# Accumulator sums by ScalarE copies and accumulating DMAs, and more seven-product places, in a hybrid encoder layer's feed-forward part

## The chip, the cores and the metric

One core of a Trainium2 chip runs the whole layer as one program. The metric is the device time of one execution in microseconds. Engines: TensorE (PE) multiplies, VectorE (DVE) and ScalarE (ACT) do elementwise work, GpSimd (POOL) and SyncE (SP) here mostly issue DMAs or do little.

## The reference

One layer on 256 tokens of width 2048 in float32. An RMSNorm and an input projection feed a gated linear recurrence and a differential attention, whose outputs go through W_out to the residual. The part that the change touches is what follows:

```python
h = rmsnorm(x, norm_ffn_w[l])
u = jax.nn.silu(jnp.einsum('bsd,df->bsf', h, w_gate[l])) * jnp.einsum('bsd,df->bsf', h, w_up[l])
x = x + jnp.einsum('bsf,fd->bsd', u, w_down[l])
```

The inner width D_FF is 5632, that is 11 chunks of 512 columns.

## The kernel before

**Products in split precision.** Every weight tile of 128x1024 float32 (two slices of 128 rows by 512 columns, a "unit") is split into a high part `whi`, a rounded copy by ACT (L134), and a rest `wlo` by a DVE subtraction (L135). Activations are split likewise, and each product is three matmuls of 128x128 by 128x512: hi by hi, hi by lo, lo by hi (L772 to L774). The class `Stream` loads units with DMAs on SP's queue into `raw` (5 buffers), and splits them in a fixed order of `items`, up to three items ahead of use, five in the feed-forward part (`HL_BUFS` and `HL_MORE` buffers). Splits have high priority in the planner, which simulates the program to fix the order on each engine.

**Seven products in place of eight.** In the feed-forward part two chunks of columns (gate and up of a chunk f; two neighbouring chunks of down) are multiplied together by `pair_product`. The contraction is done in places i of two 128-row slices. A plain place has 2 chunks x 2 halves of tokens x 2 slices = 8 products, 24 matmuls. A place named in `S_UP` or `S_DOWN` uses seven products (21 matmuls), from sums of the activations, made once, and sums of the weights: four DVE operations of 128x512 (L127, L128, L131, L132) and, besides the first unit, one half unit and two units more to split, all made in place in `raw`. Some products go to accumulators x (one per chunk and half of tokens), others to the four accumulators m, which are added to several x results at the end. Places up to the last seven come in order of i for both chunks; the remaining plain places come for chunk 0 and then for chunk 1.

**Accumulators.** The four x and four m fill all eight PSUM banks. `new_pair_accs` swaps roles from one pair to the next, so that the next pair starts in banks that m held, while x is taken out of the others.

**fold** runs after the last seven of a pair. For gate and up it forms the four sums of m into the SBUF tiles u and v: an ACT copy of m[0] (L862) and four DVE additions (L863 to L866). At the chunk's end DVE adds x[0] into u (L870), ACT takes Silu (L871), DVE adds x[1] into v (L873) and multiplies (L874). For down, fold adds the sums to the residual `xsb` with an ACT copy and eight DVE additions (L888, L890), and four more add x at the end (L903); in the second phase the result is stored from there.

**put_u** is a generator in a queue `side`, which `pump` moves on by one step after every second product. It regroups u: two DVE transposes (L405), four stores to a DRAM tile `via`, `settle(2)` (it yields until two more items are taken), one load to `ut`, a longer settle, then the split into u_hi (ACT, L836) and u_lo (DVE, L838) and the activation sums for the places in `S_DOWN` (L719 to L728). `put_sums` does the latter for the places in `S_UP` at the start of the feed-forward part. `acts.wait(i)` pumps until place i is ready.

**Phases.** Chunks 0 to 5 of gate and up, then down over their 12 places, for two pairs of column chunks; then chunks 6 to 10 and down over their 10 places.

Of the kernel before, what the change touches and what calls it, by code (L numbers as in the profile page):

```python
# [11 lines left out]
F32 = mybir.dt.float32  # L12
F32R = mybir.dt.float32r
BF16 = mybir.dt.bfloat16
U8 = mybir.dt.uint8
AF = mybir.ActivationFunctionType
ALU = mybir.AluOpType
# [3 lines left out]
P = 128  # L21
SEQ = 256
TT = SEQ // P
NC = 512
# [10 lines left out]
RAW_BUFS, HL_BUFS, HAT_BUFS = 5, 3, 5  # L35
HL_MORE = 2
PHASES = 2
S_UP = (2, 4)
S_DOWN = ((1, 3, 5, 7), (1, 3, 5))
EVERY_IN, EVERY_OUT, EVERY_FFN, WIDTH = 1, 1, 2, 2  # L40
LB_FLOOR = 1e-30
LB_CEIL = 1.0 - 1e-6
LEVELS = [1, 2, 4, 8, 16, 32, 64]
# [8 lines left out]
def encoder_layer(ctx: ExitStack, tc: tile.TileContext, xT, xr, w_in, w_out, w_gate, w_up, w_down,  # L52
# [188 lines left out]
            stream.split(upto)  # L241


    ident = const.tile([P, P], F32, name="ident")
    make_identity(nc, ident)
    nhalf = const.tile([P, 8], F32, name="nhalf")
    nc.gpsimd.memset(nhalf, -0.5)
    dist_sb = const.tile([P, TT, SEQ], F32, name="dist_sb")
    masks_sb = const.tile([P, len(LEVELS), P], U8, name="masks_sb")
    vec = const.tile([P, params.shape[1]], F32, name="vec")  # L250
    nfw = vec[:, 0:NK]
    onw, qnw, kn1, slw = (vec[:, NK + i:NK + i + 1] for i in range(4))
# [137 lines left out]
    def settle(n):  # L390

        u = stream.at
        for _ in range(2 * HPC * n):
            yield
            if stream.at >= u + n:
                break
# [428 lines left out]
    nkp = max(len(p) for p in phases) * HPC  # L825
    n_down = max(len(s) for s in S_DOWN)

    def put_u(f, u, ph, u_hi, u_lo, us_hi, us_lo, ready):

        tmp, ut = (ffn.tile([P, NQ, HPC, TT, Q], F32, tag="ut", name=n) for n in ("uq", "ut"))  # L830
        yield from regroup(ut, u, tmp)
        k0 = (f - phases[ph][0]) * HPC
# [18 lines left out]
    for ph, fs in enumerate(phases):  # L851
# [3 lines left out]
        for f in fs:  # L855
            x, m = new_pair_accs()
            u = ffn.tile([P, TT, NC], F32, tag="u", name="u")
            v = ffn.tile([P, TT, NC], F32, tag="v2", name="v", bufs=1)

            def fold():  # L860
                tt = nc.vector.tensor_tensor
                nc.scalar.copy(out=u[:, 0, :], in_=m[0])  # L862
                tt(out=u[:, 1, :], in0=u[:, 0, :], in1=m[2], op=ALU.add)  # L863
                tt(out=v[:, 0, :], in0=u[:, 1, :], in1=m[1], op=ALU.add)
                tt(out=u[:, 1, :], in0=u[:, 1, :], in1=m[3], op=ALU.add)
                tt(out=v[:, 1, :], in0=u[:, 1, :], in1=m[1], op=ALU.add)  # L866

            pair_product(up_plan[f], h_acts, x, m, EVERY_FFN, fold)
            for tt in range(TT):
                nc.vector.tensor_tensor(out=u[:, tt, :], in0=u[:, tt, :], in1=x[0][tt], op=ALU.add)  # L870
                nc.scalar.activation(out=u[:, tt, :], in_=u[:, tt, :], func=AF.Silu, scale=rstd2[:, tt:tt + 1])  # L871
            for tt in range(TT):
                nc.vector.tensor_tensor(out=v[:, tt, :], in0=v[:, tt, :], in1=x[1][tt], op=ALU.add)  # L873
                nc.vector.scalar_tensor_tensor(out=u[:, tt, :], in0=v[:, tt, :], scalar=rstd2[:, tt:tt + 1],  # L874
                                               in1=u[:, tt, :], op0=ALU.mult, op1=ALU.mult)
            side.append(put_u(f, u, ph, u_hi, u_lo, us_hi, us_lo, ready))

        u_acts = Acts(u_hi, u_lo, us_hi, us_lo, S_DOWN[ph])
        u_acts.ready = ready
        for cp in range(NCH_D // 2):  # L880
# [1 line left out]
            xs = [[xsb[:, tt, (2 * cp + c) * NC:(2 * cp + c + 1) * NC] for tt in range(TT)] for c in range(2)]  # L882

            def fold():
                t = ffn.tile([P, NC], F32, tag="v2", name="t", bufs=1)

                def add(to, what):
                    nc.vector.tensor_tensor(out=to, in0=to, in1=what, op=ALU.add)  # L888

                nc.scalar.copy(out=t, in_=m[0])  # L890
                add(xs[0][0], t)
                add(t, m[2])
                add(xs[1][0], t)
                add(xs[1][0], m[1])
                add(t, m[3])
                add(xs[0][1], t)
                add(xs[1][1], t)
                add(xs[1][1], m[1])

            pair_product(down_plan[ph, cp], u_acts, x, m, EVERY_FFN, fold)  # L900
            for c in range(2):
# [58 lines left out]
```

## Time and profile before

| | |
|---|---|
| median of 3 runs | 1227.65 us (1225.65 to 1227.96) |
| the profiled execution | 1226.58 us, its span 1224.5 us |
| PE busy | 1211.1 us (99%), 5553 matmuls |
| DVE busy | 985.9 us (81%) |
| ACT busy | 707.9 us (58%) |
| POOL busy | 38.0 us (3%) |
| DMA | 252.51 MB, mean 206 GB/s |

The span is cut into stretches to read it: the mixing part runs until about 520 us, chunks of gate and up until 778, down until 902, chunks again until 1119, and down until the end. A group's mean time is one instruction's own duration; DVE starts the next before the last has drained, so the distance between two starts is shorter.

### The profile page before, as it was taken

The numbers are of one execution on the slowest core, as the hardware profiler recorded it, in microseconds if no ns is written. First come the engines' busy times: TensorE is split into PE (matmuls) and PEld (weight loads), VectorE is DVE, ScalarE is ACT, GpSimd is POOL, SyncE is SP. The second block draws the span as 40 slices with busy tenths as digits, with TensorE's granted clock in tenths as the row PEclk, the third lists the DMA queues.
The fourth block names the chain that finished last, engine by engine and source line by source line (L and its number), as shares of the span: only waits on it lengthen the run. The fifth ranks groups of instructions, "written<-read, shape, count | busy, mean of one in ns | idle before, by whom it ended". The sixth has DMA issues, their size and how long they took to land.

```text
span 1224.5 us, 15730 instructions
## 1 busy us (share of the span) xinstructions
PE 1211.1 (99%) x5553; PEld 1000.5 (82%) x5553; DVE 985.9 (81%) x1413; ACT 707.9 (58%) x1029; POOL 38.0 (3%) x42
## 2 busy tenths in 40 slices
PE   9999999999999999999999999999999999999998
PEld 6878888887888788878888888888888888888887
DVE  6558977756987776698998988898978989888885
ACT  6657756776775665565554565464545545654542
POOL 0000111000001100000000000000000000000000
PEclk9999999999999999999999999999999999999999
DMA  8965456566445554547666675665657666766763
GB/s 308 314 229 179 150 174 205 189 211 202 149 147 186 190 184 161 188 139 255 240 201 216 227 253 196 222 223 185 216 196 239 203 212 229 253 197 222 232 208 120
DMA packets 79934, 252.51 MB, mean 206 GB/s; under 512 B 8944, under 2 KB 19824, under 8 KB 79856
## 3 DMA queue, kind: packets, MB, share of 16 engines
q1 hardware_dynamic: 79712, 251.52, 61.4%
q8 instruction: 43, 0.70, 0.2%
q14 instruction: 35, 0.29, 0.1%
q10 hardware_dynamic: 144, 0.01, 0.0%
HBM read 238.38 MB, written 13.11 MB: 205 GB/s over the span
## 4 chain that ended last, share of the span: by engine, by line
PE 85%; DMA 6%; DVE 4%; ACT 2%; issue 1%; SPq 1%; POOL 0%; ACTq 0%; DVEq 0%
PE x L773 15%; PE x L774 15%; PE x L772 15%; PE acc L377 9%; PE acc L378 9%; PE acc L376 9%; PE sc L493 2%; PE m L773 2%; PE m L774 2%; PE m L772 2%; DVE wlo L135 2%; DMA zt<-via 2%; DMA raw<-in_w_in 2%; ACT whi L134 1%; DMA ut<-via 1%
## 5 line engine op out<-in xcount | busy, mean ns | idle before, releaser
L134 ACT CAST whi<-raw 128x1024 fp32r<-128x1024 f32 (+1 forms) x497 | 498.2, 1018 | 392.0 <-PE x L774 123.2
L135 DVE TENSOR_TENSOR wlo<-raw,whi 128x1024 fp32r<-128x1024 f32 (+1 forms) x497 | 578.9, 1180 | 156.0 <-ACT whi L134 152.6
L774 PE MATMUL x<-whi,h_lo 128*128 128x512 f32 x594 | 231.2, 389 | 0.0
L773 PE MATMUL x<-wlo,h_hi 128*128 128x512 f32 x594 | 231.1, 389 | 0.0
L772 PE MATMUL x<-whi,h_hi 128*128 128x512 f32 x594 | 220.4, 389 | 0.0
L377 PE MATMUL acc<-wlo,h_hi 128*128 128x512 f32 x512 | 203.2, 397 | 2.9 <-DVE wlo L135 2.9
L378 PE MATMUL acc<-whi,h_lo 128*128 128x512 f32 x512 | 200.4, 393 | 0.0
L376 PE MATMUL acc<-whi,h_hi 128*128 128x512 f32 x512 | 193.5, 399 | 2.6 <-ACT whi L134 2.5
L772 PEld LDWEIGHTS x<-whi,h_hi 128*128 128x128 f32 x594 | 111.5, 188 | 23.3 <-ACT whi L134 0.2
L773 PEld LDWEIGHTS x<-wlo,h_hi 128*128 128x128 f32 x594 | 111.5, 188 | 23.3
L774 PEld LDWEIGHTS x<-whi,h_lo 128*128 128x128 f32 x594 | 111.5, 188 | 23.1
L377 PEld LDWEIGHTS acc<-wlo,h_hi 128*128 128x128 f32 x512 | 96.8, 189 | 24.3 <-DVE wlo L135 6.1
L376 PEld LDWEIGHTS acc<-whi,h_hi 128*128 128x128 f32 x512 | 96.1, 189 | 22.6 <-ACT whi L134 4.2
L378 PEld LDWEIGHTS acc<-whi,h_lo 128*128 128x128 f32 x512 | 96.7, 189 | 19.3
L773 PE MATMUL x<-wlo,u_hi 128*128 128x512 f32 x282 | 109.8, 389 | 0.0
L774 PE MATMUL x<-whi,u_lo 128*128 128x512 f32 x282 | 109.7, 389 | 0.0
L772 PE MATMUL x<-whi,u_hi 128*128 128x512 f32 x282 | 105.1, 390 | 0.4 <-ACT whi L134 0.4
L772 PEld LDWEIGHTS x<-whi,u_hi 128*128 128x128 f32 x282 | 52.6, 188 | 12.4 <-ACT whi L134 1.6
L773 PEld LDWEIGHTS x<-wlo,u_hi 128*128 128x128 f32 x282 | 52.9, 188 | 11.3 <-DVE wlo L135 0.4
L774 PEld LDWEIGHTS x<-whi,u_lo 128*128 128x128 f32 x282 | 52.9, 188 | 10.9
L377 PE MATMUL acc<-wlo,m_hi 128*128 128x512 f32 x128 | 50.2, 393 | 0.5 <-DVE wlo L135 0.5
L378 PE MATMUL acc<-whi,m_lo 128*128 128x512 f32 x128 | 49.9, 390 | 0.0
(192 smaller groups left out, 1289.9 us busy)
## 6 DMA issues: line engine op xcount, KB each, us to landing
raw<-in_w_in SPq DMA_DIRECT2D x127, 512.0 KB, 4.2
raw<-in_w_gate SPq DMA_DIRECT2D x88, 512.0 KB, 4.7
raw<-in_w_up SPq DMA_DIRECT2D x88, 512.0 KB, 4.7
raw<-in_w_down SPq DMA_DIRECT2D x88, 512.0 KB, 4.7
raw<-in_w_out SPq DMA_DIRECT2D x32, 512.0 KB, 4.0
via<-uq SPq DMA_DIRECT2D x44, 128.0 KB, 2.4
ut<-via SPq DMA_DIRECT2D x11, 512.0 KB, 3.3
via<-zq SPq DMA_DIRECT2D x40, 128.0 KB, 3.7
```

What stands on the lines that cost most here:

```text
L134: nc.scalar.copy(out=hi[:, k, :], in_=raw[:, k, :])
L135: self.last_split = tt(out=lo[:, k, :], in0=raw[:, k, :], in1=hi[:, k, :].bitcast(F32), op=ALU.subtract)
L376: nc.tensor.matmul(out=acc, lhsT=hi, rhs=whi[:, k, :], start=first, stop=False)
L377: nc.tensor.matmul(out=acc, lhsT=hi, rhs=wlo[:, k, :], start=False, stop=False)
L378: nc.tensor.matmul(out=acc, lhsT=lo, rhs=whi[:, k, :], start=False, stop=last)
L493: nc.tensor.matmul(out=sc[:, j, :], lhsT=kk[:, j * P:(j + 1) * P], rhs=qq(j), start=True, stop=True)
L772: nc.tensor.matmul(out=acc, lhsT=hi, rhs=whi[:, k, :], start=first, stop=False)
L773: nc.tensor.matmul(out=acc, lhsT=hi, rhs=wlo[:, k, :], start=False, stop=False)
L774: nc.tensor.matmul(out=acc, lhsT=lo, rhs=whi[:, k, :], start=False, stop=left[id(acc)] == 0)
```

## The change

More places use seven products: `S_UP` goes from (2, 4) to (1, 3, 5), `S_DOWN` from (1, 3, 5, 7) and (1, 3, 5) to (1, 3, 5, 7, 9) and (1, 3, 5, 7). In fold of gate and up, ACT copies m[1] into both halves of v; DVE makes two sums; two accumulating DMAs on POOL's queue add them into v. At the chunk's end ACT copies x[0] to a new tile xg and one accumulating DMA adds it into u. Silu and the multiplication move into put_u, behind a new settle(2). In down's fold four DVE additions remain and four accumulating DMAs add the sums to `xsb`. Three constant tiles move to the pool `mixp`, whose memory the feed-forward pool takes over.

```diff
-S_UP = (2, 4)
-S_DOWN = ((1, 3, 5, 7), (1, 3, 5))
+S_UP = (1, 3, 5)
+S_DOWN = ((1, 3, 5, 7, 9), (1, 3, 5, 7))
...
-    ident = const.tile([P, P], F32, name="ident")
+    ident = mixp.tile([P, P], F32, name="ident")
...
-    dist_sb = const.tile([P, TT, SEQ], F32, name="dist_sb")
-    masks_sb = const.tile([P, len(LEVELS), P], U8, name="masks_sb")
+    dist_sb = mixp.tile([P, TT, SEQ], F32, name="dist_sb")
+    masks_sb = mixp.tile([P, len(LEVELS), P], U8, name="masks_sb")
...
-    def put_u(f, u, ph, u_hi, u_lo, us_hi, us_lo, ready):
+    def put_u(f, u, v, ph, u_hi, u_lo, us_hi, us_lo, ready):
+        yield from settle(2)
+        for tt in range(TT):
+            rs = rstd2[:, tt:tt + 1]
+            with tc.issue_after(stream.last_split.ins):
+                nc.scalar.activation(out=u[:, tt, :], in_=u[:, tt, :], func=AF.Silu, scale=rs)
+            nc.vector.scalar_tensor_tensor(out=u[:, tt, :], in0=v[:, tt, :], scalar=rs, in1=u[:, tt, :],
+                                           op0=ALU.mult, op1=ALU.mult)
+            yield
...
             def fold():
                 tt = nc.vector.tensor_tensor
+                t = ffn.tile([P, NC], F32, tag="sm", name="t")
                 nc.scalar.copy(out=u[:, 0, :], in_=m[0])
-                tt(out=u[:, 1, :], in0=u[:, 0, :], in1=m[2], op=ALU.add)
-                tt(out=v[:, 0, :], in0=u[:, 1, :], in1=m[1], op=ALU.add)
-                tt(out=u[:, 1, :], in0=u[:, 1, :], in1=m[3], op=ALU.add)
-                tt(out=v[:, 1, :], in0=u[:, 1, :], in1=m[1], op=ALU.add)
+                for c in range(2):
+                    nc.scalar.copy(out=v[:, c, :], in_=m[1])
+                tt(out=t, in0=u[:, 0, :], in1=m[2], op=ALU.add)
+                tt(out=u[:, 1, :], in0=t, in1=m[3], op=ALU.add)
+                nc.gpsimd.dma_start(out=v[:, 0, :], in_=t, accum_op=ALU.add)
+                nc.gpsimd.dma_start(out=v[:, 1, :], in_=u[:, 1, :], accum_op=ALU.add)
             pair_product(up_plan[f], h_acts, x, m, EVERY_FFN, fold)
+            xg = ffn.tile([P, TT, NC], F32, tag="ut", name="xg")
             for tt in range(TT):
-                nc.vector.tensor_tensor(out=u[:, tt, :], in0=u[:, tt, :], in1=x[0][tt], op=ALU.add)
-                nc.scalar.activation(out=u[:, tt, :], in_=u[:, tt, :], func=AF.Silu, scale=rstd2[:, tt:tt + 1])
+                nc.scalar.copy(out=xg[:, tt, :], in_=x[0][tt])
+            nc.gpsimd.dma_start(out=u, in_=xg, accum_op=ALU.add)
             for tt in range(TT):
                 nc.vector.tensor_tensor(out=v[:, tt, :], in0=v[:, tt, :], in1=x[1][tt], op=ALU.add)
-                nc.vector.scalar_tensor_tensor(out=u[:, tt, :], in0=v[:, tt, :], scalar=rstd2[:, tt:tt + 1],
-                                               in1=u[:, tt, :], op0=ALU.mult, op1=ALU.mult)
...
             def fold():
-                t = ffn.tile([P, NC], F32, tag="v2", name="t", bufs=1)
...
-                nc.scalar.copy(out=t, in_=m[0])
-                add(xs[0][0], t)
-                add(t, m[2])
-                add(xs[1][0], t)
-                add(xs[1][0], m[1])
-                add(t, m[3])
-                add(xs[0][1], t)
-                add(xs[1][1], t)
-                add(xs[1][1], m[1])
+                t = ffn.tile([P, 2, NC], F32, tag="v2", name="t12", bufs=1)
+                t3 = ffn.tile([P, NC], F32, tag="sm", name="t3")
+                tt = nc.vector.tensor_tensor
+                nc.scalar.copy(out=t[:, 0, :], in_=m[0])
+                tt(out=t[:, 1, :], in0=t[:, 0, :], in1=m[2], op=ALU.add)
+                tt(out=t3, in0=t[:, 1, :], in1=m[3], op=ALU.add)
+                for c in range(2):
+                    tt(out=xs[1][c], in0=xs[1][c], in1=m[1], op=ALU.add)
+                for to, what in ((xs[0][0], t[:, 0, :]), (xs[1][0], t[:, 1, :]), (xs[0][1], t3), (xs[1][1], t3)):
+                    nc.gpsimd.dma_start(out=to, in_=what, accum_op=ALU.add)
```

## Rows read from the trace of the kernel before

**Rows 1.** The page: its head and the busy time of each engine.

```profile
span 1224.5 us, 15730 instructions
PE 1211.1 (99%) x5553; PEld 1000.5 (82%) x5553; DVE 985.9 (81%) x1413; ACT 707.9 (58%) x1029; POOL 38.0 (3%) x42
```

**Rows 2.** Busy time by stretch (columns in the first line): gate/up chunk, down pattern, down product.

```profile
core 0: us, PE busy (x) PEld busy (x) DVE busy (x) ACT busy (x) POOL busy (x), PEclk, DMA share, GB/s
567.19:609.35 42.16, 42.16 (x187) 34.91 (x186) 37.90 (x48) 22.87 (x26) 0.00 (x0) 1.00 0.67 227
...
778.00:818.80 40.80, 40.59 (x179) 33.05 (x178) 37.45 (x44) 22.04 (x25) 0.00 (x0) 1.00 0.58 192
840.00:902.50 62.50, 62.50 (x277) 51.74 (x277) 53.26 (x60) 32.23 (x33) 0.00 (x0) 1.00 0.61 204
```

**Rows 3.** Waits of five gate/up chunks, 567.19 to 778: who for whom, us, times, longest.

```profile
ACT whi L134 <- PE x L774: 35.0, 26, 1.8
...
ACT u_hi L836 <- DMA ut<-via: 11.8, 5, 2.5
ACT whi L134 <- DMA raw<-in_w_up: 8.0, 12, 1.4
DVE s L719 <- DMA ut<-via: 4.5, 4, 1.2
DVE u_lo L838 <- ACT u_hi L836: 3.6, 5, 2.1
```

**Rows 4.** DVE in order of time: start, us, what. Splits, four chained additions, two additions.

```profile
546.75 5.76 DVE L135 TENSOR_TENSOR wlo<-raw,whi 128x1024 fp32r<-128x1024 f32 x5
...
628.76 0.69 DVE L127 TENSOR_TENSOR raw<-raw 128x512 f32<-128x512 f32 x1
...
631.55 4.88 DVE L135 TENSOR_TENSOR wlo<-raw,whi 128x1024 fp32r<-128x1024 f32 x4
...
831.24 0.68 DVE L903 TENSOR_TENSOR xsb<-x,xsb 128x512 f32<-128x512 f32 x1
831.84 0.68 DVE L888 TENSOR_TENSOR xsb<-xsb,m 128x512 f32<-128x512 f32 x1
```

**Rows 5.** Groups by line and shape, 560 to 1180: busy us, mean ns of one.

```profile
L134 ACT CAST whi<-raw 128x1024 fp32r<-128x1024 f32 x266 | 274.2, 1051 | 237.1 <-DVE raw L128 99.4 <-PE x L774 91.4 <-DMA raw<-in_w_up 16.4
...
L728 DVE TENSOR_TENSOR us_lo<-s,us_hi 128x384 fp32r<-128x384 f32 x7 | 3.9, 551 | 0.0
...
L719 DVE TENSOR_TENSOR s<-ut 128x128 f32<-128x128 f32 x7 | 2.0, 292 | 7.8 <-DMA ut<-via 7.8
```

**Rows 6.** The page, DMA issues: KB each, median us from issue to landing.

```profile
raw<-in_w_gate SPq DMA_DIRECT2D x88, 512.0 KB, 4.7
...
via<-uq SPq DMA_DIRECT2D x44, 128.0 KB, 2.4
ut<-via SPq DMA_DIRECT2D x11, 512.0 KB, 3.3
```

**Rows 7.** One chunk in order of time, ACT and then DVE: fold and the additions into v.

```profile
591.41 0.57 ACT L862 COPY u<-m 128x512 f32<-128x512 f32 x1
...
596.98 0.68 DVE L864 TENSOR_TENSOR v<-u,m 128x512 f32<-128x512 f32 x1
...
609.35 1.28 DVE L873 TENSOR_TENSOR v<-v,x 128x512 f32<-128x512 f32 x2
```

**Rows 8.** First chunk: busy time of a stretch, then rows of PE, ACT and DVE.

```profile
523.10:552.40 29.30, 27.77 (x128) 22.16 (x127) 28.60 (x47) 19.11 (x30) 1.12 (x1) 1.00 0.44 143
...
534.19 1.03 PE L702 MATMUL tpx<-ident,xsb 128*128 128x128 f32 x8
...
531.26 0.51 ACT L727 CAST hs_hi<-s 128x384 fp32r<-128x384 f32 x1
...
540.93 0.87 DVE L707 SCALAR_TENSOR_TENSOR h_lo<-tpx,vec,h_hi 128x256 fp32r<-128x256 f32 x2
```

**Rows 9.** The last operation of DVE.

```profile
1220.25 0.69 DVE L903 TENSOR_TENSOR xsb<-x,xsb 128x512 f32<-128x512 f32 x1 [0.67 <-PE x L774]
```

More of the change, by code (lines that the diff above doesn't have):

```diff
@@ L861, in fold @@
                 tt = nc.vector.tensor_tensor
+                t = ffn.tile([P, NC], F32, tag="sm", name="t")
                 nc.scalar.copy(out=u[:, 0, :], in_=m[0])
-                tt(out=u[:, 1, :], in0=u[:, 0, :], in1=m[2], op=ALU.add)
-                tt(out=v[:, 0, :], in0=u[:, 1, :], in1=m[1], op=ALU.add)
-                tt(out=u[:, 1, :], in0=u[:, 1, :], in1=m[3], op=ALU.add)
-                tt(out=v[:, 1, :], in0=u[:, 1, :], in1=m[1], op=ALU.add)
+                for c in range(2):
[4 more added lines that the diff above has]
+                nc.gpsimd.dma_start(out=v[:, 1, :], in_=u[:, 1, :], accum_op=ALU.add)
             pair_product(up_plan[f], h_acts, x, m, EVERY_FFN, fold)
+            xg = ffn.tile([P, TT, NC], F32, tag="ut", name="xg")
             for tt in range(TT):
-                nc.vector.tensor_tensor(out=u[:, tt, :], in0=u[:, tt, :], in1=x[0][tt], op=ALU.add)
-                nc.scalar.activation(out=u[:, tt, :], in_=u[:, tt, :], func=AF.Silu, scale=rstd2[:, tt:tt + 1])
+                nc.scalar.copy(out=xg[:, tt, :], in_=x[0][tt])
+            nc.gpsimd.dma_start(out=u, in_=xg, accum_op=ALU.add)
             for tt in range(TT):
                 nc.vector.tensor_tensor(out=v[:, tt, :], in0=v[:, tt, :], in1=x[1][tt], op=ALU.add)
-                nc.vector.scalar_tensor_tensor(out=u[:, tt, :], in0=v[:, tt, :], scalar=rstd2[:, tt:tt + 1],
-                                               in1=u[:, tt, :], op0=ALU.mult, op1=ALU.mult)
-            side.append(put_u(f, u, ph, u_hi, u_lo, us_hi, us_lo, ready))
+            side.append(put_u(f, u, v, ph, u_hi, u_lo, us_hi, us_lo, ready))
         u_acts = Acts(u_hi, u_lo, us_hi, us_lo, S_DOWN[ph])
@@ L884, in fold @@
             def fold():
-                t = ffn.tile([P, NC], F32, tag="v2", name="t", bufs=1)
-                def add(to, what):
-                    nc.vector.tensor_tensor(out=to, in0=to, in1=what, op=ALU.add)
-                nc.scalar.copy(out=t, in_=m[0])
-                add(xs[0][0], t)
-                add(t, m[2])
-                add(xs[1][0], t)
-                add(xs[1][0], m[1])
-                add(t, m[3])
-                add(xs[0][1], t)
-                add(xs[1][1], t)
-                add(xs[1][1], m[1])
+                t = ffn.tile([P, 2, NC], F32, tag="v2", name="t12", bufs=1)
[8 more added lines that the diff above has]
+                    nc.gpsimd.dma_start(out=to, in_=what, accum_op=ALU.add)
             pair_product(down_plan[ph, cp], u_acts, x, m, EVERY_FFN, fold)
```

## The prediction

> **What bounds the kernel now.** I read the page's busy shares first [rows 1]: TensorE (PE) is busy 1211.1 of 1224.5 us, VectorE (DVE) 985.9, ScalarE (ACT) 707.9. An average hides stages, so next the busy time by stretch [rows 2], where the granted clock is 1.00 throughout. One chunk of gate and up takes 42.16 us, all of it PE, and DVE works 37.90 us of it (90%). A product of down takes 62.50 us, again all PE, with 53.26 us of DVE (85%). Then the waits inside five such chunks [rows 3]: PE waits for nothing there; ACT waits 35.0 us for PE to give split buffers back, so the split of weights runs as far ahead as its buffers allow. PE sets the time by the number of its matmuls, and DVE is the next limit, 4.3 us per chunk behind.
>
> **What the change takes from PE.** At one place of the two-chunk product the seven-product step needs 21 matmuls where the plain one needs 24. A chunk of gate and up has 8 places, two of them sevens: 8 x 24 - 2 x 3 = 186 matmuls in 42.16 us, 0.2267 us each. A third seven takes 3 away in each of 11 chunks (33). Down gets one more seven in each of 4 products (two phases, two pairs of columns): 12. So 45 matmuls go, 45 x 0.2267 = 10.2 us, if PE stays the bound. A chunk would then be 41.48 us, a long product 61.8.
>
> **What it puts on DVE.** Back to back, a 128x1024 split subtraction follows the last one after 1.135 us (five in 5.76 us, the last lasting 1.22) and 128x512 additions follow each other every 0.60 us; the four additions that make a seven's weight sums take 2.79 us together, being chained [rows 4]. A plain place costs DVE 2 x 1.135 = 2.27 us; a seven 3 x 1.135 + 0.60 + 2.79 = 6.8 us, against 21 x 0.2267 = 4.76 us of PE. Each new seven adds 4.5 us. The relief in a gate/up chunk: the four additions of fold become two, the two of x[0] go to ACT copies and a DMA: four fewer, 4 x 0.60 = 2.4 us. In down, eight additions of fold become four: again 2.4 us. The Silu, the multiplication and the transposes are moved, not removed. Two more pairs of u need sums over 11 chunks, some 1.5 to 2 us each by their rows (five of 0.29, one of 0.55, overlapping; [rows 5]), 0.3 us per chunk. So DVE per gate/up chunk: 37.9 + 4.5 - 2.4 + 0.3 = 40.3 of 41.48 us (97%), 1.2 us left over. Per long product of down: 53.3 + 2.1 = 55.4 of 61.8 us (90%). Down is safe; gate and up sit on the edge.
>
> Is 97% enough to keep PE fed? The nearest stretch of the old trace with sevens at every second place is the start of down: four sevens and four plain places in 40.80 us, DVE 37.45 busy (92%), PE idle for 0.21 us [rows 2]. That pattern holds with five split buffers. I take 0.2 us of PE waits for each of the other ten gate/up chunks, 2 us in all (bounds: 0, and 1.6 us a chunk if DVE's waits for the regrouped u, 4.5 + 3.6 us in five chunks [rows 3], can no longer be hidden), and nothing in down.
>
> **ACT.** Per gate/up chunk: one and a half split casts more (1.05 and half of it, [rows 5]), two copies of m[1] and two of x[0] (0.57 each, [rows 7]): 22.9 + 1.6 + 2.3 = 26.8 of 41.5 us. It costs nothing while ACT is ahead of DVE; the cover is that third of idle time.
>
> **The new transfers.** Three accumulating DMAs per chunk on POOL's queue (two of 256 KB into v, one of 512 KB into u), four of 256 KB per product of down. The old trace has no accumulating DMA and none issued by POOL. Nearest rows: a 128 KB store to DRAM lands in 2.4 us, a 512 KB load of the regrouped u in 3.3, a 512 KB weight load in 4.7 [rows 6]; I take 4 us, bounds 2.4 and 8 (read and write of the target, twice the 4 us). Who waits: (a) the addition of x[1] into v on DVE; queued behind it are weight splits, and PE behind those. The last seven now ends 4 plain units, 48 matmuls or 10.9 us, before the chunk's end (before: 72, 16.3 us). Fold's second addition came 5.6 us after the copy of m[0] [rows 7], since splits go first; so the second DMA starts at about -5 us, lands near -1 with 4 us and near +3 with 8, and the v additions came right at the chunk's end in the old order [rows 7]. (b) Silu on ACT waits for u; x[0] is complete 24 matmuls (5.4 us) before the end, its copies and DMA take some 1.2 + 4 us, and Silu stands behind settle(2), about 5.4 us after the end: free. (c) POOL's queue is in order, but otherwise empty here. SP's queue keeps its four stores and one load per chunk; they come later by settle(2), and so does u's completion: its 24 pump turns, two slots of 3 matmuls each, take 144 matmuls, and the earliest place of down that needs the last chunk now comes after 180 (phase 1) or 225 (phase 0). Free. The raw-load traffic is the same; 1 MB more per 41.5 us is 25 GB/s beside 224 [rows 2].
>
> By the Trainium skill (DMA: Bandwidth & Descriptors, Anatomy of one DMA) a transfer of POOL's queue takes some 2.0 us plus its bytes at 436 GB/s, 2.6 us for 256 KB as an estimate; by it (a) would be hidden as well. No run here shows it yet.
>
> **PSUM.** The first sevens of the next chunk reuse the banks of x. x[0] and x[1] had 48 matmuls (10.9 us) after the chunk's end before the next m needs a bank, now 24 (5.4 us), and m[3] after 36 (8.2 us). Copies and additions of 0.6 us fit unless (a) is late.
>
> **The first chunk** is where I expect a loss. From 523.1 to 552.4 us DVE is busy 28.60 of 29.30 us and PE already waits 1.5 us [rows 8]. To get through its third seven, the new order needs 6.8 us more of DVE for 4.8 more of PE, and a third set of activation sums (0.6 + 0.8 + 0.7 = 2.1 us): 4.1 us short. Also ident, dist and masks move to memory that the feed-forward pool takes over; sums that land there wait for the last transposes, which ran at 534.19 while hs_hi was first written at 531.26 [rows 8]. And the tp banks for m[2], m[3] come free at 541.8 after those transposes, while the first seven now comes 5.4 us earlier. I take +4 us, bounds 0 and 9 (4.1 + 5).
>
> **The end.** After the last seven of down 10.9 us remain, with no splits to make beyond those already issued; four additions (2.4 us) and four DMAs fit. The last two additions wait for PE as they do now [rows 9]. Zero; if the last transfer lands late, some 4 us.
>
> **Sum.** -10.2 + 4 + 2 = -4.2 us. On the profiled execution, 1226.58 us (span 1224.5 and 2.1 around it), that is 1222.4; this execution is 1.1 us below the median 1227.65, so I give 1223.4.
>
> **Rivals.**
> *Full saving:* PE never waits, 1227.65 - 10.2 = 1217.4. For it: the alternating stretch of down lost 0.21 us. Against it: the first chunk. 12%.
> *DVE becomes the bound by its own waits.* Its waits for the regrouped u stay (1.6 us a chunk), 40.3 + 1.6 = 41.9 us a chunk, or up to the old 42.16 with waits for casts whose load is late (ACT waited 8.0 us for weights of up in five chunks [rows 3]). Ten chunks at -0.26 to 0 us, down -2.7, first chunk +4 - 0.7: 1225.6 to 1228.3. 22%.
> *The accumulating DMA is late (slower).* One place: DVE stands at v's addition with splits behind it. With L us of wait a chunk is 41.9 + L; the total is -2.0 + 10 L us. It is slower than before by more than 2.5 us from L = 0.45. The longest DVE wait for a transfer in those chunks is 1.2 us [rows 3]: 1227.65 + 10.0 = 1237.7. For it: transfers in this kernel already land later than the order assumed (u_hi waited 11.8 us in five chunks). Against it: 10.9 us of room. 26%.
> The Trainium skill (SBUF — State Buffer, Who interferes with whom) speaks for this rival: VectorE and GpSimd share SBUF ports, an operation with two SBUF inputs blocks a GpSimd operation that reads SBUF, and a DMA of POOL's queue is late while its descriptors can't be written. It infers that a tensor_tensor leaves descriptor writing alone, which would leave L at 0; no trace here shows which holds.
>
> **Chances and range.** Forecast 40%, and 12, 22 and 26% for the rivals. About 0.2% (2.5 us) is what a measurement can tell from no change. Faster: 0.40 + 0.12 = 0.52; same 0.22; slower 0.26. The forecast alone spans 1218.5 to 1225; the range goes from the full saving, 1217, to L = 1.0, 1236; outside it I leave some 5% below and 12% above.
>
> **What the new profile would show.** 5508 matmuls instead of 5553, spaced 0.227 us where PE is the bound. Gate/up chunks of 41.5 to 41.7 us with DVE at 40 us; if they are 42 or longer with PE waiting for whi or wlo, the DVE rivals hold, and the waits of DVE tell which: on the regrouped u, or on a DMA into v. In the first chunk, PE waits of some 5 us. I am wrong if accumulating DMAs take over 8 us, or if PE's gaps outside the first chunk come to more than 5 us.

## The result and the profile after

The changed kernel is 6.8% slower: 1310.55 us median of 4 runs (1306.45 to 1315.56) against 1226.65 (1225.25 to 1227.96) for the kernel before beside it, ratio 1.0679, 95% interval 1.0651 to 1.0707. The forecast was 1223.4 us, the range 1217 to 1236. The profiled execution took 1308.86 us, with a span of 1307.0.

The page of the changed kernel, against [rows 1]: head, busy time, and POOL's DMA queue (packets, MB, share of 16 engines).

```profile
span 1307.0 us, 15933 instructions
...
PE 1242.2 (95%) x5508; PEld 1000.6 (77%) x5508; DVE 1017.1 (78%) x1462; ACT 749.2 (57%) x1109; POOL 81.1 (6%) x91
...
q0 software_dynamic: 7056, 15.73, 6.7%
```

Its DMA issues, against [rows 6]: KB each, median us from issue to landing.

```profile
u<-xg POOLq DMA_DIRECT2D x11, 512.0 KB, 4.8
via<-uq SPq DMA_DIRECT2D x44, 128.0 KB, 3.0
ut<-via SPq DMA_DIRECT2D x11, 512.0 KB, 6.4
...
xsb<-t POOLq DMA_DIRECT2D x16, 256.0 KB, 7.5
v<-t POOLq DMA_DIRECT2D x11, 256.0 KB, 7.6
v<-u POOLq DMA_DIRECT2D x11, 256.0 KB, 8.9
```

The 45 matmuls are gone (5508), and still the span is 82.5 us longer. PE stands idle for 1307.0 - 1242.2 = 64.8 us where it stood for 13.4, and it is busy 31.1 us longer in spite of the 45, part of it at half the clock (below). No other engine is at its limit: DVE's share fell from 81 to 78%.

Busy time by stretch, against [rows 2]: two gate/up intervals from fold to fold, the long product of down, and 9 us around one gap of PE (the column after POOL is the granted clock).

```profile
core 0: us, PE busy (x) PEld busy (x) DVE busy (x) ACT busy (x) POOL busy (x), PEclk, DMA share, GB/s
...
656.00:705.07 49.07, 43.65 (x184) 33.80 (x184) 40.37 (x51) 26.19 (x33) 2.64 (x3) 1.00 0.71 215
705.07:753.50 48.43, 45.45 (x183) 36.16 (x184) 38.54 (x49) 25.71 (x33) 2.62 (x3) 0.93 0.71 217
...
870.39:932.59 62.20, 62.15 (x275) 51.14 (x274) 55.85 (x63) 32.79 (x37) 3.52 (x4) 1.00 0.72 223
...
628.00:633.36 5.36, 1.43 (x5) 0.86 (x5) 2.25 (x5) 2.32 (x4) 0.00 (x0) 0.74 0.74 183
633.36:636.77 3.41, 3.41 (x8) 2.57 (x9) 3.41 (x4) 3.31 (x4) 0.00 (x0) 0.50 0.32 91
```

The long product of down is as forecast: 62.20 us, PE busy throughout. A gate/up interval is 49 us where 41.5 was forecast, although DVE works 38.5 to 40.4 us in it, just the 40.3 of the prediction. So the sum of DVE's work was right, and DVE spends 9 to 10 us of each interval waiting. After a gap of PE the clock sits at half (0.50, 1.2 GHz): eight matmuls take 3.41 us, 1.81 at the full clock's 0.2267 each.

Waits of the whole execution: who for whom, us in total, times, longest; the line by itself is of the kernel before. There PE hardly waited, and ACT's casts stood for PE to give buffers back [rows 3] and for the weight sums.

```profile
POOL u L883 <- DMA v<-u: 69.4, 9, 9.0
ACT u L834 <- DMA u<-xg: 60.5, 10, 8.7
...
ACT u_hi L844 <- DMA ut<-via: 40.8, 11, 4.2
...
PE m L772 <- ACT whi L134: 31.7, 27, 3.7
...
DVE u L835 <- ACT u L834: 29.1, 11, 3.8
...
ACT whi L134 <- PE x L774: 25.0, 27, 2.7
...
DVE v L885 <- DMA v<-u: 17.9, 10, 3.0
...
DVE v L885 <- DMA v<-t: 5.6, 5, 1.9
```

```profile
ACT u_hi L836 <- DMA ut<-via: 25.8, 11, 2.5
```

Now PE waits for casts (31.7 us), and the casts stand behind operations that wait for transfers: Silu for u<-xg, the split u_hi for the regrouped u (40.8 us, 25.8 before), and on DVE the additions into v (17.9 + 5.6). One chunk's end, each engine in order of time: POOL, DVE, ACT, PE (start, us, what, and in brackets the idle time before and what ended it).

```profile
664.75 0.87 POOL L876 DMA_DIRECT2D v<-t  x1 [37.64 <-ACT whi L134]
665.47 1.05 POOL L877 DMA_DIRECT2D v<-u  x1
675.47 0.87 POOL L883 DMA_DIRECT2D u<-xg  x1 [8.95 <-DMA v<-u]
...
672.40 0.69 DVE L885 TENSOR_TENSOR v<-v,x 128x512 f32<-128x512 f32 x1 [1.94 <-DMA v<-t]
...
675.00 0.69 DVE L885 TENSOR_TENSOR v<-v,x 128x512 f32<-128x512 f32 x1 [1.31 <-DMA v<-u]
675.61 0.68 DVE L128 TENSOR_TENSOR raw<-raw 128x512 f32<-128x512 f32 x1
...
680.75 1.41 DVE L835 SCALAR_TENSOR_TENSOR u<-v,rstd,u 128x512 f32<-128x512 f32 x2 [1.88 <-ACT u L834]
...
676.40 1.05 ACT L134 CAST whi<-raw 128x1024 fp32r<-128x1024 f32 x1 [6.67 <-DVE raw L128]
679.99 1.33 ACT L834 ACTIVATE u<-u,rstd 128x512 f32<-128x512 f32 x2 [2.54 <-DMA u<-xg]
681.23 4.39 ACT L134 CAST whi<-raw 128x1024 fp32r<-128x1024 f32 x5
...
682.31 0.50 PE L772 MATMUL m<-whi,hs_hi 128*128 128x512 f32 x1 [2.19 <-ACT whi L134]
```

Fold's two DMAs are issued at 664.75 and 665.47. v's addition on DVE waits for each, the second one landing 9.5 us after its issue. The weight sum L128 of the next seven is behind it on DVE, and a cast on ACT behind that (6.67 us idle). The DMA into u reads nothing of v, but u[:, 1] is the source of v<-u, so POOL holds it for 8.95 us until that transfer has landed; for the last 6.5 of them xg had been ready (ACT's second copy of x[0] was over at 669.0). Silu then stands on ACT for u<-xg, the next seven's casts wait behind Silu, and PE waits 2.19 us for the first of them.

Where the 82.5 us lie, by the distances between the ACT copies of m[0] that begin each fold, less the matmuls in between at 0.2267 us [rows 2] (the third column is the run after_no_dma below):

| | before | after | after without the DMAs |
|---|---|---|---|
| start to the first fold, later than before, less its 21 matmuls more (4.8) | 0 | 10.0 | 7.6 |
| nine gate/up intervals: beyond their matmuls | 5.2 | 66.5 | 30.2 |
| two passages from gate/up into down | 2.1 | 16.3 | 10.4 |
| products of down, passage back | -1.9 | 5.8 | -0.5 |

(10.0 + 88.6 - 5.4 - 10.2 is 83.0, and the end gives 0.4 back: 82.6, with roundings.)

### The profile page after: what moved, and what is told of

It is laid out like the page before. It is cut to its first block, busy times and chain, and to the rows that moved or that the text cites. A ratio compares the mean times of both kernels' runs of the same rounds, so it can differ in the third digit from the quotient of the medians.

```text
span 1307.0 us, 15933 instructions
## 1 busy us (share of the span) xinstructions
PE 1242.2 (95%) x5508; PEld 1000.6 (77%) x5508; DVE 1017.1 (78%) x1462; ACT 749.2 (57%) x1109; POOL 81.1 (6%) x91
## 5 line engine op out<-in xcount | busy, mean ns | idle before, releaser
L134 ACT CAST whi<-raw 128x1024 fp32r<-128x1024 f32 (+1 forms) x527 | 515.4, 1005 | 347.9 <-DVE raw L128 132.1
L135 DVE TENSOR_TENSOR wlo<-raw,whi 128x1024 fp32r<-128x1024 f32 (+1 forms) x527 | 600.0, 1165 | 138.2 <-ACT whi L134 134.4
L773 PE MATMUL x<-wlo,h_hi 128*128 128x512 f32 x539 | 213.7, 397 | 4.5 <-DVE wlo L135 4.4
L774 PE MATMUL x<-whi,h_lo 128*128 128x512 f32 x539 | 212.2, 394 | 0.0
L772 PE MATMUL x<-whi,h_hi 128*128 128x512 f32 x539 | 203.5, 408 | 5.8 <-ACT whi L134 5.7
L773 PEld LDWEIGHTS x<-wlo,h_hi 128*128 128x128 f32 x539 | 103.1, 191 | 29.7 <-DVE wlo L135 7.8
L774 PEld LDWEIGHTS x<-whi,h_lo 128*128 128x128 f32 x539 | 103.1, 191 | 21.5
L772 PE MATMUL x<-whi,u_hi 128*128 128x512 f32 x262 | 96.3, 396 | 0.4 <-ACT whi L134 0.4
L772 PE MATMUL m<-whi,hs_hi 128*128 128x512 f32 x99 | 37.0, 431 | 27.3 <-ACT whi L134 27.3
L773 PE MATMUL m<-wlo,hs_hi 128*128 128x512 f32 x99 | 43.5, 439 | 8.4 <-DVE wlo L135 8.4
```

The lines of the kernel that those rows point to most:

```text
L134: nc.scalar.copy(out=hi[:, k, :], in_=raw[:, k, :])
L135: self.last_split = tt(out=lo[:, k, :], in0=raw[:, k, :], in1=hi[:, k, :].bitcast(F32), op=ALU.subtract)
L772: nc.tensor.matmul(out=acc, lhsT=hi, rhs=whi[:, k, :], start=first, stop=False)
L773: nc.tensor.matmul(out=acc, lhsT=hi, rhs=wlo[:, k, :], start=False, stop=False)
L774: nc.tensor.matmul(out=acc, lhsT=lo, rhs=whi[:, k, :], start=False, stop=left[id(acc)] == 0)
```

## Experiments

Each run has the kernel before beside it, at 1225.9 to 1227.5 us; "+" figures are differences of medians. "Interval" is the mean of the nine gate/up distances from fold to fold: 42.7 us before, 48.9 after. Where no ratio is given the kernel ran once, and a few us between two such runs tell nothing.

### Each half alone

**dmas_only** is the changed kernel with the old places of sevens; **dmas_const** is that with the three constant tiles in their old pool too.

```diff
-S_UP = (1, 3, 5)
-S_DOWN = ((1, 3, 5, 7, 9), (1, 3, 5, 7))
+S_UP = (2, 4)
+S_DOWN = ((1, 3, 5, 7), (1, 3, 5))
```

> The changed kernel with the old places (S_UP 2, 4; S_DOWN as before): copies, accumulating DMAs and moved Silu alone. Late transfers: DVE does 35.5 us of work per chunk and stands some 4.7 us at v and behind Silu and 2 us at the regrouped u, 42.2 us against PE's 42.16, so at most a few us are lost: 1227 to 1240. Rival, the transfers hurt by themselves (they slow the weight loads, or ACT's stand stops the casts for longer than five buffers cover): 1260 or more.

> Copies, accumulating DMAs and moved Silu with the old places and all constants in const. If the stands behind the transfers cost 6 us a chunk by themselves: first fold near 544, chunks 48 us, 1286 to 1291. If the late start of the feed-forward part made the chunks slow as well: under 1270.

dmas_only took 1300.59 us (+74.6, ratio 1.0603, interval 1.0561 to 1.0646), dmas_const 1290.05 (+64.2, 1.0538, 1.0505 to 1.0571), with intervals of 48.4 and 49.0 us. So 64 to 75 of the 84 us come without any new seven, although DVE has less to do than before (in dmas_const 948.5 us busy in all, 74%).

**no_dma_old_places** takes only the DMAs out of dmas_const and keeps the ACT copies and the moved Silu and product.

```diff
-                nc.gpsimd.dma_start(out=v[:, 0, :], in_=t, accum_op=ALU.add)
-                nc.gpsimd.dma_start(out=v[:, 1, :], in_=u[:, 1, :], accum_op=ALU.add)
...
-            nc.gpsimd.dma_start(out=u, in_=xg, accum_op=ALU.add)
...
-                for to, what in ((xs[0][0], t[:, 0, :]), (xs[1][0], t[:, 1, :]), (xs[0][1], t3), (xs[1][1], t3)):
-                    nc.gpsimd.dma_start(out=to, in_=what, accum_op=ALU.add)
```

> The changed kernel's order with Silu and the product moved, but the old places (two sevens in gate and up) and the old places of the three constant tiles, and without the accumulating DMAs: the sums that these would add are left out of v, u and xsb. Theory 1 (the third seven is what lengthens a chunk to 45 us where no transfer is waited for): chunks at their matmuls, 42.2 to 42.6 us, and 1220 to 1230 us in all. Rival (the Silu and the product moved behind settle(2) are what costs): chunks of 44 us or more and about 1245.

It took 1229.27 us (+1.8, 1.0024, 1.0005 to 1.0043), interval 43.1. One interval of dmas_const and one of this run, busy time:

```profile
1060.09:1107.14 47.05, 43.23 (x187) 34.60 (x187) 35.23 (x44) 24.46 (x31) 2.62 (x3) 1.00 0.70 224
```

```profile
1057.26:1099.38 42.12, 42.12 (x188) 34.83 (x187) 35.56 (x41) 24.91 (x32) 0.00 (x0) 1.00 0.69 225
```

The same work on every engine but POOL, 4.9 us apart. The copies and the moved steps cost some 1.8 us; the transfers cost 64.2 - 1.8 = 62 us at the old places. This run takes out two things at once: the traffic, and the waits of Silu and v's addition for it. Without u<-xg Silu no longer needs x[0] and may run before x[0] is copied.

**sevens_only** is the kernel before with the new places and constant tiles, and no transfer.

```diff
-S_UP = (2, 4)
-S_DOWN = ((1, 3, 5, 7), (1, 3, 5))
+S_UP = (1, 3, 5)
+S_DOWN = ((1, 3, 5, 7, 9), (1, 3, 5, 7))
...
-    ident = const.tile([P, P], F32, name="ident")
+    ident = mixp.tile([P, P], F32, name="ident")
...
```

> The new S_UP and S_DOWN and the moved constants in the kernel before, with all sums on DVE and no accumulating DMA. Late transfers (theory): without them a gate/up chunk is bound by DVE's own work, 37.9 + 4.5 + 0.3 = 42.7 us, or 44.3 with its waits for the regrouped u, so some 1232 to 1250 us in all and no long stands on ACT's Silu. Rival, too many sevens: the split of weights itself can't follow, whatever makes the sums, and this kernel is about as slow as the changed one (1290 to 1330) or slower, since DVE has 2.4 us more per chunk.

1276.28 us (+50.3, 1.0405, 1.0375 to 1.0435), interval 46.3: more than the 1250 that I allowed for. Without the relief DVE has 37.9 + 4.5 + 0.3 = 42.7 us to do in 41.5, but 46.3 is more than that. The new places cost on their own, and the two halves don't add (64 + 50 against 84). That the later one counts where both make the same casts late is my reading; no run shows it.

### What about the transfers costs

**dmas_plain** turns the accumulating DMAs of dmas_const into plain copies, which overwrite v, u and xsb. **dmas_settle5** puts Silu and the product later. **dmas_own_tile** gives v<-u a source of its own, so that u<-xg needn't wait for it.

```diff
-                nc.gpsimd.dma_start(out=v[:, 0, :], in_=t, accum_op=ALU.add)
+                nc.gpsimd.dma_start(out=v[:, 0, :], in_=t)
...
```

```diff
-        yield from settle(2)
+        yield from settle(5)
```

```diff
+                t2 = ffn.tile([P, NC], F32, tag="sm", name="t2")
+                nc.scalar.copy(out=t2, in_=u[:, 1, :])
-                nc.gpsimd.dma_start(out=v[:, 1, :], in_=u[:, 1, :], accum_op=ALU.add)
+                nc.gpsimd.dma_start(out=v[:, 1, :], in_=t2, accum_op=ALU.add)
```

> Copies, transfers and moved Silu with the old places, all constants in const, but plain copying DMAs on POOL's queue in place of accumulating ones (so what they should add overwrites). If the accumulation makes them late (it reads its target too): they land some us earlier and the time falls well under 1290, to 1240 to 1265. If the queue and the program's place for the waiting operations make them late: 1280 to 1295.

> Copies, accumulating DMAs and moved Silu with the old places, all constants in const, Silu behind settle(5) in place of settle(2), some 8 us later in the program. If ACT's stand at Silu (6 us a chunk) is what costs: it goes, and the time falls from 1290 to 1240 to 1260 (the stands at v and the regrouped u stay). If Silu's stand was covered by other slack: 1285 to 1295.

> Copies, transfers and moved Silu with the old places and constants in const; ACT copies the second sum to a tile of its own, and the DMA into v reads that, so the DMA into u no longer waits in POOL's queue until the one that reads u has landed (6 to 9 us). If that queue is what makes u late: Silu's stand shrinks from 6 us to 1 or 2, 1290 falls to 1250 to 1270. If u is late in any case: 1280 to 1295.

| | us | interval | v<-t, v<-u, u<-xg land after | ACT stands for u<-xg, for ut<-via |
|---|---|---|---|---|
| dmas_const | 1290.05 | 49.0 | 7.4, 8.1, 8.2 | 64.5, 36.5 |
| dmas_own_tile | 1279.88 | 47.5 | 7.6 (both v), 8.8 | 55.6, 35.1 |
| dmas_settle5 | 1254.45 | 45.1 | 8.5, 9.4, 7.5 | 65.7, 3.3 |
| dmas_plain | 1250.61 | 45.2 | 4.8, 5.7, 7.0 | 37.6, 34.4 |

Two of ACT's waits, of the whole execution, in dmas_const and then in dmas_settle5: Silu for its transfer, and the split u_hi for the regrouped u.

```profile
ACT u L834 <- DMA u<-xg: 64.5, 10, 8.9
...
ACT u_hi L844 <- DMA ut<-via: 36.5, 11, 4.2
```

```profile
ACT u L834 <- DMA u<-xg: 65.7, 10, 8.8
...
ACT u_hi L844 <- DMA ut<-via: 3.3, 7, 1.4
```

As plain copies v's transfers land 2.5 us sooner and u's 1.2, which gives back 39 us of the 62; Silu's stand falls from 64.5 to 37.6 us, and that of the product behind it on DVE from 47.5 to 20.8. settle(5) gives back 36, but not through Silu, which stands as long as before. What goes there is the second stand of a chunk, that of u_hi. So Silu and u_hi both stand in front of casts, and taking away much of either gives back more than half; the two gains overlap (39 + 36 against 62). v's addition waits for no transfer at the old places; what waits for v's transfers there is POOL with u<-xg. That hold is worth 10 us only; with its own source u<-xg lands 8.8 us after its issue instead.

**v_by_dve** and **u_by_dve** take one of the two back to DVE in the changed kernel.

```diff
...
-                nc.gpsimd.dma_start(out=v[:, 0, :], in_=t, accum_op=ALU.add)
-                nc.gpsimd.dma_start(out=v[:, 1, :], in_=u[:, 1, :], accum_op=ALU.add)
...
+                tt(out=v[:, 0, :], in0=u[:, 1, :], in1=m[1], op=ALU.add)
...
+                tt(out=v[:, 1, :], in0=u[:, 1, :], in1=m[1], op=ALU.add)
```

```diff
-            xg = ffn.tile([P, TT, NC], F32, tag="ut", name="xg")
...
-                nc.scalar.copy(out=xg[:, tt, :], in_=x[0][tt])
-            nc.gpsimd.dma_start(out=u, in_=xg, accum_op=ALU.add)
+                nc.vector.tensor_tensor(out=u[:, tt, :], in0=u[:, tt, :], in1=x[0][tt], op=ALU.add)
```

> The changed kernel, but the four sums of m in gate and up by DVE as before, no accumulating DMA into v; x[0] still by ACT copies and a DMA into u. Late transfers: DVE no longer stands at v (2.1 us a chunk) and the DMA into u no longer queues behind the one that reads u, so Silu's stand (6 us a chunk) goes too; DVE work is 41.5 us a chunk: some 1230 to 1250. If Silu still stands for several us, the DMA into u is late by itself and the time stays above 1260.

> The changed kernel, but x[0] added into u by DVE, no xg and no DMA into u; the accumulating DMAs into v stay. Late transfers: the stands at v remain (2 to 3 us a chunk), those behind Silu go (2.6 us on DVE, 6 on ACT); DVE work 41.5 us: 43.5 to 46 us a chunk, 1245 to 1270. Rival, too many sevens: 1290 or more, as the changed kernel.

1273.45 us (+47.5, interval 45.6) and 1290.9 (+65.0, 46.4). Of the 84 us, v's transfers are worth about 36 and u's about 19. Without u's transfer the wait for v<-u doesn't vanish: it passes to DVE's addition into u, which overwrites that transfer's source and stands 28.3 us for it.

**idle_paced** is the kernel before with four unread 256 KB accumulating DMAs per chunk, at about the times of the real ones and with none in down (three constant tiles make room for theirs in mixp).

```diff
+    def pace(col):
+        p = ffn.tile([P, 1], F32, tag="pace", name="pace", bufs=6)
+        nc.scalar.copy(out=p, in_=col)
+        nc.gpsimd.tensor_copy(out=idle[:, 0, 0:1], in_=p)
...
+                for _ in range(2):
+                    nc.gpsimd.dma_start(out=idle[:, 1, :], in_=idle[:, 0, :], accum_op=ALU.add)
...
```

> As the kernel with idle accumulating DMAs beside the old sums, but paced without DVE: ACT copies one column (of v after fold, of u at the chunk's end) to a small tile of its own, POOL copies it on, so DVE waits for nothing of POOL. If those 70 us came from DVE's wait for POOL (16.7 us in three and a half chunks at L881): 1226 to 1235, chunks of 42.2 to 43 us. If accumulating DMAs slow the kernel with no waiter at all: chunks of 45 us or more, 1255 or more.

1243.46 us (+16.6), interval 43.8. Busy time of the stretch 610 to 780, where the kernel before has 170.00 us of PE and a DMA share of 0.65:

```profile
610.00:780.00 170.00, 169.32 (x743) 138.65 (x743) 149.67 (x182) 91.53 (x111) 18.15 (x24) 1.00 0.80 246
```

The DMA share rises to 0.80 and PE loses 0.7 us of 170: plain traffic is nearly free there. The loss is spread: in the profiled execution 4.6 us in the first chunk of each phase (49.0 and 47.0 us, 47.7 and 43.6 before), 5.3 in the other seven gate/up intervals, 5.7 in the two passages into down. ACT stands 41.6 us for the regrouped u here, 25.8 before, so traffic, with the pacing, can have up to 16.6 us of the loss. Nor are these transfers quite like the real ones: POOL issues each when the last has landed (one at 606.36, the next at 612.79), where the two into v are in flight together. An earlier form, idle_dmas, let POOL read a column of v and u directly; DVE then waited 16.7 us for POOL between 600 and 760, so its 1297.27 us measure the pacing in the main.

> The kernel before, with as many bytes of accumulating DMAs per gate/up chunk as the changed one has (four of 256 KB, paced by a one-column POOL copy of v after fold and of u at the chunk's end), into a tile that nobody reads. Late transfers: nobody waits, so 1226 to 1230. Contention (they slow weight loads, or POOL and DVE block each other): 1240 or more, or DVE operations visibly longer than 0.69 and 1.22 us.

### Why three sevens cost without any transfer

**after_no_dma** is the changed kernel without the DMAs, with ident back in its old pool.

> The changed kernel (ident in const) without its accumulating DMAs: the sums into v, u and xsb are left out, all else stays (new places, copies, moved Silu, the additions that remain). Late transfers alone: nothing stands any more, DVE has 40.3 us of work per 41.5 us chunk and the time is 1216 to 1232. Too many sevens: with no transfer at all the chunks still take 44 us or more, because splits and weight loads can't be fed at three sevens in a row, 1250 or more.

1258.39 us (+31.5), interval 44.8, with DVE busy some 39 us of it: DVE is not full, and no wait for a POOL transfer is left; u_hi still stands 37.4 us for the regrouped u. Three runs start from it: a sixth raw buffer (**no_dma_raw6**; for its memory the long products of down have three sevens less and the short ones two, 30 matmuls or 6.8 us more), a longer distance to u's regrouping (**no_dma_far6**), and other places for the three sevens (**no_dma_246**).

```diff
-S_DOWN = ((1, 3, 5, 7, 9), (1, 3, 5, 7))
+S_DOWN = ((1, 3), (1, 3))
...
-                raw = wpool.tile([P, KU, NC], F32, tag="raw", name="raw", bufs=RAW_BUFS)
+                if self.nr and self.nr % (RAW_BUFS + 1) == 0:
+                    raw = self.more.tile([P, KU, NC], F32, tag="raw2", name="raw", bufs=1)
+                else:
+                    raw = wpool.tile([P, KU, NC], F32, tag="raw", name="raw", bufs=RAW_BUFS)
...
```

```diff
-        yield from regroup(ut, u, tmp)
+        yield from regroup(ut, u, tmp, 6)
```

```diff
-S_UP = (1, 3, 5)
+S_UP = (2, 4, 6)
```

> The changed kernel without transfers, gate and up with three sevens, and a sixth raw buffer in the feed-forward part (for its memory, down has only places 1 and 3 as sevens, which adds 5 x 3 x 2 = 30 matmuls, 6.8 us; the sums into v, u and xsb stay left out). Only the gate/up chunks are compared: without the sixth buffer they take 45.0 us. If weight loads that wait for a raw buffer hold up the sevens: 42 to 43.5 us. If the late regrouped u does: still 44.5 to 45.5.

> The changed kernel without transfers, with regroup's last settle 6 in place of 3, so that the split of the regrouped u stands about 8 us later in the program. If ACT's stand of 3 to 4 us and DVE's of 2 us there cost the chunk its 3.5 us over 41.5: 42 to 43 us a chunk, 1225 to 1235 in all. If loads of weights do: 44.5 to 45.5 and 1250 to 1260. The planner may also place it no later than before; then the stands are still there and nothing follows.

> The changed kernel without the accumulating DMAs (the sums that they would add are left out) and ident back in its old place, as in an earlier run of 1258.4 us with chunks of 45.0 us; here the three sevens of gate and up stand at places 2, 4 and 6 in place of 1, 3 and 5. There the four chained additions for the first seven stood 7.4 us instead of 2.8 us on DVE, since the additions into v and the products of the chunk before came between them. Theory 1 (the first seven at place 1 meets the end of the chunk before): at place 2 it has 24 matmuls, 5.4 us, more room, and chunks fall to 43 us or less, 1240 us or less in all. Rival (DVE's load over the whole chunk, or the number of raw buffers, decides, wherever the sevens stand): 44.5 to 45.5 us a chunk and about 1255.

1247.35 us (+20.5, interval 43.0), 1259.18 (+32.3, 44.8) and 1239.48 (+12.0, ratio 1.0106, 1.0075 to 1.0137, interval 43.3). no_dma_far6 doesn't test the regrouping: u_hi stands 40.3 us in it, no less than without the edit. The other places give back 19 us. The four chained sums of a chunk's first seven on DVE, and the casts on ACT that follow them, first in after_no_dma (place 1), then in no_dma_246 (place 2):

```profile
615.56 0.69 DVE L127 TENSOR_TENSOR raw<-raw 128x512 f32<-128x512 f32 x1
...
616.90 0.68 DVE L882 TENSOR_TENSOR v<-v,x 128x512 f32<-128x512 f32 x1
...
618.63 0.74 DVE L835 SCALAR_TENSOR_TENSOR u<-v,rstd,u 128x512 f32<-128x512 f32 x1
...
622.29 0.68 DVE L132 TENSOR_TENSOR raw<-raw 128x512 f32<-128x512 f32 x1
...
623.09 4.42 ACT L134 CAST whi<-raw 128x1024 fp32r<-128x1024 f32 x5 [4.94 <-DVE raw L132]
```

```profile
618.78 1.41 DVE L835 SCALAR_TENSOR_TENSOR u<-v,rstd,u 128x512 f32<-128x512 f32 x2
...
621.96 0.69 DVE L127 TENSOR_TENSOR raw<-raw 128x512 f32<-128x512 f32 x1
...
624.14 0.69 DVE L132 TENSOR_TENSOR raw<-raw 128x512 f32<-128x512 f32 x1
...
623.49 1.05 ACT L134 CAST whi<-raw 128x1024 fp32r<-128x1024 f32 x1 [3.29 <-DVE raw L128]
624.94 2.10 ACT L134 CAST whi<-raw 128x1024 fp32r<-128x1024 f32 x2 [0.40 <-DVE raw L132]
```

At place 1 the sums take 6.73 us from L127 to L132, because the additions into v and the products of the chunk before come between them, and ACT stands 4.94 us; at place 2 they are over before the sums begin, the sums take 2.18 us, and ACT stands 3.29 us before the first cast of the seven (0.31 at place 1) and 0.40 behind the last sum. Over the execution ACT's waits for L132 fall from 44.0 to 11.5 us and those for L128 rise from 123.0 to 133.8; u_hi's stand falls too, from 37.4 to 21.1. So the places are shown to be worth 19 us, but which of these stands carries it is not. In no_dma_raw6 ACT waits 40.3 us behind the last sum, nearly as in after_no_dma, and its interval is 43.0 all the same: that fits casts that run further ahead with a buffer more. What is left in no_dma_246 (an interval 0.5 us longer than before in spite of three matmuls less, 8 us in the first chunk) was not taken further.

### The first chunk, and down alone

**ident_moved** is the kernel before with ident in the pool mixp; **after_ident** is the changed kernel with ident back in const (and lprod moved for it).

```diff
-    ident = const.tile([P, P], F32, name="ident")
+    ident = mixp.tile([P, P], F32, name="ident")
```

> The kernel before with one line changed: ident lives in the pool mixp, whose memory the feed-forward pool takes over. In the kernel with the transfers and the old places the first r (L813) started at 537.5 us, right after the last transposes that read ident, where before it was 526.9. If the moved ident is the cause of the late first fold (556.7 against 543.7): 10 to 13 us slower in all, the other chunks unchanged at 42.2 us. If that came from the transfers: as before, 1226.

> The changed kernel with ident back in const (lprod goes to mixp in its place). If ident's memory costs by itself: first fold earlier by 8 to 10 us and 1299 to 1303 in all; chunks still 49 us. If the first chunk is slow for want of DVE alone: as the changed kernel, 1306 to 1315.

1231.98 us (+6.1, 1.0061, 1.0031 to 1.0091), the first fold at 551.2 instead of 543.7; but 1309.53 (+83.7), the first fold at 558.0 instead of 558.5. The wait for ident's memory is real. A row of DVE in dmas_only, whose counterpart ran at 526.88 without a wait before:

```profile
537.51 0.69 DVE L813 TENSOR_TENSOR r<-h_hi,h_lo 128x512 f32<-128x512 f32 x1 [4.50 <-PE tpx L702]
```

With three sevens it is hidden behind DVE's other excess there: without it, and without the DMAs, the first fold is still 7.6 us late.

**down_ident** is the kernel before with the new S_DOWN alone, dist and masks moved to mixp for it.

```diff
-S_DOWN = ((1, 3, 5, 7), (1, 3, 5))
+S_DOWN = ((1, 3, 5, 7, 9), (1, 3, 5, 7))
```

> The kernel before with the new S_DOWN alone, all sums on DVE, ident in const (dist and masks moved). Down products of 61.8 us were reached by every kernel so far with five sevens in phase 0. If sevens are free there: 12 matmuls fewer, 2.7 us, 1223 to 1226. If DVE at 93% loses them: 1226 to 1235.

1224.78 us (1222.69 to 1228.97, 8 runs; before 1225.87 beside it), ratio 0.9992, 0.9974 to 1.0010: no difference that this measurement can show, though the best time of all. The long product of down by itself:

```profile
826.41:888.28 61.87, 61.87 (x275) 51.23 (x274) 57.91 (x67) 33.10 (x36) 0.00 (x0) 1.00 0.65 207
```

Five sevens run there without a gap of PE and with all sums on DVE (57.91 of 61.87 us). The 2.7 us that twelve matmuls are worth is about the size of the uncertainty.

## Why the prediction was wrong

**What was right.** PE as the bound and its price per matmul; DVE's load (40.3 us said, 38.5 to 40.4 read); down's long product at 61.8 us (62.2 read, 61.87 in down_ident; only the last product of the second phase is longer, 55.9 us against 51.7 by its 228 matmuls); nothing at the end (0.4 us less). The third rival named the right kind of mechanism, the late accumulating DMA in front of splits, and gave it 26%.

**First failed step: "I take 4 us, bounds 2.4 and 8".** The 256 KB transfers into v land after 7.6 and 8.9 us in the median, the second over 9 us in the chunk shown. The rows near it were loads and stores of 128 to 512 KB [rows 6]; none of them accumulates, and the same transfers as plain copies land after 4.8 and 5.7 us. So 4 us was close for what the rows showed and half of what the accumulating ones into v take here. Accumulating isn't all of it: u<-xg, with twice the bytes, landed after 4.8 us in the changed kernel, and the unread transfers, one at a time, after 5.8 in idle_paced and 3.5 in idle_dmas. By the Trainium skill (DMA: Bandwidth & Descriptors, Anatomy of one DMA) a 256 KB transfer of this queue comes to 2.6 us as an estimate; the measured 7.6 and 8.9 us are about three times that, and they decide.

**Second failed step: (b) Silu "free", and (c) POOL's queue "otherwise empty" and u's completion "Free".** I placed u<-xg 5.4 us before the chunk's end by when x[0] is complete, and checked the queue's load but not the dependences among its own entries: u<-xg may not overwrite u[:, 1] until v<-u is done, so POOL waits 69.4 us in nine chunks and u comes after v. Then Silu stands 60.5 us on ACT in front of casts. The prediction asked who queues behind v's addition on DVE, but not who queues behind Silu; ACT's "third of idle time" was taken as cover, and it is none for a wait that blocks an in-order engine. Behind Silu the regrouped u comes late as well, and u_hi stands 40.8 us where it stood 25.8. That plain copies give 39 us back with Silu's stand shortened, and settle(5) 36 with u_hi's gone, points to both as carriers at the old places; how the 84 us of the changed kernel divide among them and v's addition is not shown. In the rival's form, 41.9 + L, an interval of 48.9 us makes L 7.0 us, where I had priced 1.2; but DVE stands only 23.5 us at v in eleven chunks, 2.1 each, so v's addition, the rival's only place, isn't the main one.

**Third failed step: "0.2 us of PE waits" a chunk for three sevens.** Without any transfer the interval is 44.8 us, 3.4 beyond its matmuls. I compared totals, 97% against the 92% of the start of down, and took down's pattern as proof. Its first seven meets the additions into v and the products as well, in the kernel before:

```profile
777.69 0.69 DVE L127 TENSOR_TENSOR raw<-raw 128x512 f32<-128x512 f32 x1
...
783.77 0.65 DVE L132 TENSOR_TENSOR raw<-raw 128x512 f32<-128x512 f32 x1
```

The sums take 6.08 us there, almost the 6.73 of after_no_dma, and PE loses 0.21 us. So one such burst costs next to nothing behind chunks with two sevens. With three sevens it returns in every chunk at the higher load, and an interval loses 3.4 us; moving the sevens to 2, 4, 6 takes 19 of the 31.5 us away, and a sixth buffer shortens the interval as much. What had no ground was to price a burst in every chunk, at 97%, by one that came once in a phase.

**First chunk: +4, bounds 0 and 9; measured +10.0, outside them.** Both mechanisms named can be seen (7.6 us are left without the DMAs and with ident in its old pool, by my reading DVE's excess; ident's memory alone costs 7.5 us to the first fold at the old places), but they overlap.

**Not in the prediction: the clock.** Mean granted clock, of the changed kernel, where before it was 0.999:

```profile
core 0: 1307.0 us, clock 0.982
```

(1 - 0.982) x 1307.0 is 23.5 us of PE's time, 1.2 before; it lies in 13 stretches at 1.2 GHz, each around or after a gap of PE as the one at 633.36 above. I had priced a gap at its own length. How much of the 22 us reaches the end is open: after_no_dma and no_dma_far6 have 0.992 and 0.997 and take 1258.39 and 1259.18 us, so there part of it lies beside waits that are due anyway.

**Left open.** Why accumulating transfers into v land later than plain ones in the same places, and whether the unread ones of idle_paced (5.8 us in the median) land sooner because they go one at a time; whether DVE's traffic delays POOL's descriptors was not tried. What makes the third seven cost in every chunk, the stand behind the sums or that of u_hi, is open too.

## What to carry to other kernels

Before moving an addition from an engine to an accumulating DMA, write down for its consumer what is queued behind it on that consumer's in-order engine, and for each transfer which earlier transfer still reads its target; a slack in busy time covers neither. Follow the moved value on to its next waits too: the regrouped u came late behind Silu. Price the transfer from a row of the same kind, beside the same traffic, or from both sides up to twice a plain copy. Where load per chunk fits only on average, look for the burst: here other places for the sevens, at the same total, gave back 19 of 31.5 us. A gap of PE was paid for a second time in the matmuls after it, at half the clock.

## What the runs showed of the hardware

An accumulating DMA of 256 KB from SBUF to SBUF on POOL's queue, one of two in flight together beside some 220 GB/s of traffic, took 7.3 to 9.4 us to land in the median of a run, a plain one in the same place 4.8 to 5.7 us; accumulating ones that were issued one at a time took 3.5 and 5.8 us. Four such transfers per chunk that nobody waits for cost PE 0.7 us in 170 us of steady chunks, with the DMA share up from 0.65 to 0.80. In a gap of PE of 3.66 us the granted clock fell to 0.50, and the eight matmuls behind the gap still ran at it, in 3.41 us where the full clock takes 1.81. POOL held a DMA back for 8.95 us until an earlier one that reads the new one's target had landed.
